# Loading the quarters of x and the first gate pair's weights during the attention heads

## The chip, the cores and the metric

The kernel runs on one core of one Trainium2 chip. The metric is the device time of the program in microseconds. TensorE (PE) multiplies, with its weight loads shown apart (PEld); VectorE (DVE), ScalarE (ACT) and GpSimd (POOL) compute elementwise; SyncE (SP) issues most of the DMAs, POOL some.

## The reference

One DeepNorm decoder layer in float32: 512 tokens, width 1024. A combined projection gives q, k, v (8 heads of 64), the input p of a pool mixer and the gates of two branches:

```python
proj = h @ w_in[l]
q, k, v, p, g = jnp.split(proj, [...], axis=-1)
y_attn = moba_attention(q.reshape(hs), k.reshape(hs), v.reshape(hs), rel_bias) @ w_branch_attn[l]
y_pool = multiscale_pool(p, w_pool_group[l], pool_scale[l]) @ w_branch_pool[l]
gates = jax.nn.sigmoid(g.astype(jnp.float32)).astype(h.dtype).reshape(B, S, N_BRANCHES, D)
mixed = gates[:, :, 0] * y_attn + gates[:, :, 1] * y_pool
h = layer_norm(ALPHA * h + mixed @ w_out[l], ln1_g[l], ln1_b[l])
a, u = jnp.split(h @ w_ffn_in[l], 2, axis=-1)
a = causal_dwconv(a, conv_w[l], conv_b[l])
f = (jax.nn.gelu(a, approximate=False) * u) @ w_ffn_out[l]
h = layer_norm(ALPHA * h + f, ln2_g[l], ln2_b[l])
```

The attention adds a relative bias per head and is causal. The change lies in the part that computes the gates and in the attention heads ahead of it; nothing of the mathematics differs.

## The kernel before, in words

Activations are kept transposed, channels on the partitions: x^T is eight tiles of 128 x 512. A product in float32 is made of three passes in a reduced type (`mm3`, L243 to L247): high x high, low x high, high x low. The high and low parts of a weight or an activation come from `split` (L72 to L78): ACT copies the high part (L76), DVE subtracts it (L77).

Many of the projections are done in pairs of output tiles by seven block products instead of eight (`seven`, L285). For that the weights of a pair are needed as four tiles A, X, D and Y, made of sums of weights. `fetch_raw` (L176) loads A and D as they are, on SP (L180, L182); X is loaded plainly on SP (L188) and then the other weights are added to it by an accumulating DMA on POOL (L190). `fetch_seven` (L194) forms Y on DVE (L207) and splits each. The activations are needed as four sums of quarters of x^T, called nT1, T3, nT2 and T4: `t_form` (L261) makes one of them in place of a quarter on DVE (L264 or L267) and, where it is told to, splits it. The weights of later chunks are fetched three chunks ahead; a pair's X and D are loaded into "homes", places that a small function gives for each pair. A home is free for the next load when the split of the pair that had it is done.

The order of the program is this:

- Input projections, in pairs, and the pool mixer. q and k of two heads each are copied out of the accumulators into the tiles `rq` and `rk` (three buffers of each).
- Eight heads (loop at L650). In step h the key and query of head h + 2 are prepared (`head`), a product that has nothing to do with heads is done as filler (`in_tile` for h < 4, a branch product `early_branch` after that, copied by DVE at L646), the scores of head h + 2 are computed (`scores`), every second step two finished heads are multiplied with v (`pv`, tile `ob`), and the probabilities of head h are transposed (`trans`, L616, with copies to `PT` on ACT and DVE, L618 to L620). In `scores` DVE finds the maxima (four instructions at L550 into `pp` and `nm`, negated at L553), ACT takes the exponentials (L556), DVE the reciprocals of the sums (L558), and POOL scales the rows (L561).
- The branch stage (L684 on): the branch outputs, oT split into high and low, and ten branch products (`br_mm`). Here the four quarters of x^T are loaded once more by four DMAs on POOL into `quad0` to `quad3` (L689); the first gate pair's X and D are loaded into `oT`, which is no longer needed by then; from the third branch product on one sum of quarters per product is formed and split.
- Six gate pairs, f = 2 to 7, by `seven`; their tiles in the profile are `sag`, `sbg` and `scg`, and the split sums are `gT` and `gnT`. X of pair f has `quad1` or `quad3` for a home, in turn, D one half of `quad2`.
- The output projection, the first LayerNorm, the gated feed-forward part and the second LayerNorm.

The order of the instructions on each engine is set by the scheduler of the language, from the dependencies, from a timeline that it estimates and from places where the program says that something may be issued only after something else (`issue_after`). A line of the program therefore says little of the place at which it is issued. The change's line numbers are five higher than these in the part on the heads.

Of the kernel before, what the change touches and what calls it, by code (L numbers as in the profile page):

```python
# [14 lines left out]
P = 128  # L15
S = 512
# [36 lines left out]
def layer_kernel(ctx: ExitStack, tc: tile.TileContext, xT, x, w_v, w_c, rel_bias, invcnt, w_group,  # L53
# [18 lines left out]
    def split(hi, lo, src, copy=None):  # L72
        if copy:
            copy(hi, src)
        else:
            state["hi"] = nc.scalar.activation(hi, src, AF.Copy)  # L76
        state["lo"] = nc.vector.tensor_tensor(lo, src, hi.bitcast(F32), op=ALU.subtract)  # L77
        return state["lo"]  # L78
# [182 lines left out]
    def t_form(n, tt, b11, b12, b21, b22, cut=True, c=slice(0, 256)):  # L261
        if n in ("nT1", "T3"):
            v, a = {"nT1": (b11, b11), "T3": (b12, b22)}[n]
            nc.vector.tensor_tensor(v, a, b12, op=ALU.subtract)  # L264
        else:
            v, a = {"nT2": (b22, b11), "T4": (b21, b22)}[n]
            nc.vector.scalar_tensor_tensor(v, a, -1.0, v, op0=ALU.mult, op1=ALU.subtract)  # L267
        if cut:
            split(*(t[:, :, c] for t in tt[n]), v)
        return v  # L270
# [43 lines left out]

    keepp = ExitStack()
    zT = keepp.enter_context(tc.tile_pool(name="keepz", bufs=1)).tile([P, 4, S], F32, name="zT")
    attn = ExitStack()
    av = attn.enter_context(tc.tile_pool(name="av", bufs=3, side="right", reuse_waits="tile"))
    strips = {}
# [9 lines left out]
    nc.gpsimd.memset(eps_t, EPS)  # L329
    dummy = const.tile([P, 1], F32, name="dummy")  # L330
    nc.scalar.activation(dummy, eps_t, AF.Copy)
    warm = const.tile([P, S], mybir.dt.bfloat16, name="warm")
    nc.vector.memset(warm, 0.0)
    wb_ = bank("warm_ps")
    for i in range(WARM):
# [187 lines left out]
    second = in_tile("p", PLAIN[1])  # L523

    def heads_done(p, ba):
        raw_q[p] = av.tile([P, S], F32, tag="rq", name=f"rq{p}")
        state["copy"] = nc.scalar.activation(raw_q[p], ba, AF.Copy)

    Ps = {}
# [35 lines left out]
    for n in range(1 + pairs):  # L565
        if n == 0:
            u, done = xr[1][:, 3, :], lambda ba, u: pool_sum(0, ba)
        else:
            u = raw_k[n - 1] = av.tile([P, S], F32, tag="rk", name=f"rk{n - 1}")
            done = lambda ba, u, p=n - 1: heads_done(p, ba)  # L570
        seven(("i", n), (xT_hi, xT_lo), ti, xr[1][:, 2, n % 2 * 256:n % 2 * 256 + 256], u, done)
        if n == 0:
            behind_sum.close()
            pool_dif(PLAIN[0], state["Y"])
            pool_sum(PLAIN[1], second)
            with tc.issue_after(state["acc"].ins):
                write_table(table)
        elif n == 1:
            pool_out(PLAIN[0])
            pool_dif(PLAIN[1], state["add"])  # L580
            pool_dif(0, state["add"])
            pool_sum(1, xr[1][:, 3, :], -1.0)
            add1 = state["add"]
        elif n == 2:
            pool_out(PLAIN[1])
            pool_dif(1, add1)
            with tc.issue_after(state["acc"].ins):
                load_strip(0)
                load_strip(1)
            head(0, state["add"], state["copy"])  # L590
        elif n == 3:
            pool_out(0)
            pool_out(1)
            head(1, state["add"], state["copy"])
            pooling.close()
            aw = attn.enter_context(tc.tile_pool(name="aw", bufs=3, side="right", reuse_waits="tile"))
            scores(0)
# [46 lines left out]
    def early_branch(f):  # L644
        t = branch[f, 1] = gates[:, 2 * GSEVEN + f, :]
        nc.vector.tensor_copy(t, br_mm(f, 1))  # L646

    scores(1)
    with tc.issue_after(exps[0].ins):
        flush()  # L650
    for h in range(H):
        if h + 2 < H:
            head(h + 2, nms[h], exps[h])
        if h < 4:
            in_tile(*fill.pop(0))
        elif h < H - 1:
            early_branch(h - 4)
        if h + 2 < H:
            scores(h + 2)
        with ExitStack() as held:  # L660
            if h and h % 2 == 0:
                pv(h // 2 - 1)
                held.enter_context(tc.issue_after(state["pv"].ins))
            trans(h)
        if h < 4:
            with tc.issue_after(nms[h].ins), tc.issue_after(exps[h].ins):
                split(zT_hi[:, h, :], zT_lo[:, h, :], zT[:, h, :])
        if h == H - 1:
            early_branch(h - 4)
    pv(H // 2 - 1)  # L670
# [6 lines left out]
    more = bp.tile([P, 4, S], F32, name="more")  # L677
    for k in range(4):
        split(oT_hi[:, k, :], oT_lo[:, k, :], oT[:, k, :])
    gxs = ExitStack()  # L680
    gx = gxs.enter_context(tc.tile_pool(name="gx", bufs=1, reuse_waits="tile"))
    tg = {"nT1": tuple(gx.tile([P, 4, 256], F32R, name=f"gnT1_{q}") for q in ("hi", "lo"))}
    gx.tile([P, 256], F32, name="gx_gap")
    qraw = [gx.tile([P, D], F32, name=f"quad{n}") for n in range(4)]  # L684
    for n in parts[1:]:
        tg[n] = tuple(gx.tile([P, 4, 256], F32R, name=f"g{n}_{q}") for q in ("hi", "lo"))
    quads = [t.rearrange("p (k t) -> p k t", k=4) for t in qraw]
    for n, (k, t) in enumerate(((k1, t1), (k1, t2), (k2, t1), (k2, t2))):
        nc.gpsimd.dma_start(quads[n], xT[k.start * P:k.stop * P, t].rearrange("(k p) t -> p k t", p=P))  # L689
    state["limit"] = WO0 - 1  # L690
    mts = {}

# [1 line left out]
        nc.gpsimd.tensor_tensor(a, b, a, op=ALU.add)  # L694
        mts[f] = a

    homes["g", "X"] = lambda f: oT[:, 0:2, :].rearrange("p a c -> p (a c)")
    homes["g", "D"] = lambda f: oT[:, 2, :]
    for q in "XD":
        coming[q].remove(("g", GSEVEN))  # L700
        fetch_raw(("g", GSEVEN), q)
        homes.pop(("g", q))

    unused = [more[:, n, :] for n in range(4)]
    forms = list(parts)
    order = [(4, 1), (5, 1), (6, 1), (6, 0)] + [(f, 0) for f in range(6)]
    for n, (f, br) in enumerate(order):
        if f < GSEVEN:
            with tc.issue_after(state["o"].ins):
                for g in range(2):  # L710
                    nc.scalar.activation(gslot[8 * g + f], gslot[8 * g + f], AF.Sigmoid)
        b = br_mm(f, br)
        if f < GSEVEN:
            for t, v in ((gslot[8 + f], branch[f, 1]), (gslot[f], b)):
                nc.vector.tensor_tensor(t, t, v, op=ALU.mult)
            merged(f, gslot[f], gslot[8 + f])
            unused += [gslot[8 + f], branch[f, 1]]
        else:
            t = branch[f, br] = unused.pop(0)
            nc.scalar.activation(t, b, AF.Copy)  # L720
        if n >= 2 and forms:
            t_form(forms[0], tg, *quads)
            forms.pop(0)
            if not forms:
                homes["g", "X"] = lambda f: qraw[1 + 2 * (f % 2)]
                homes["g", "D"] = lambda f: qraw[2][:, f % 2 * S:(f % 2 + 1) * S]

    def gate_done(f, ba, u):
        if f < KT - 1:
# [20 lines left out]
              lambda ba, u, f=f: gate_done(f, ba, u), first_half if f == KT - 1 else None)  # L750
    bz = br_mm(f, 1, last_bank[0], range(2, 4), True)
    flush()
    gxs.close()
    ext = actp.enter_context(tc.tile_pool(name="ext", bufs=1, side="right"))
    mx_hi = act.tile([P, KT, S], F32R, tag="actT_hi", name="mx_hi")
    mx_lo = act.tile([P, KT, S], F32R, tag="actT_lo", name="mx_lo")
# [428 lines left out]
```

## Time and profile before

| | |
|---|---|
| median of the runs | 641.33 us (641.03 to 643.21, 3 runs) |
| profiled execution | 640.88 us |
| its span in the trace | 639.2 us, mean granted clock of TensorE 0.99 |
| TensorE busy | 619.3 us, 97% |
| DVE, ACT, POOL busy | 511.8, 361.5, 121.3 us |
| heads | about 85 to 150 us of the span |
| branch stage | about 150 to 181 us |
| first two gate pairs | about 181 to 210 us |

In the rows of a timeline the first number is the start within the span, the second the duration, both in microseconds; at the end stands, in brackets, how long the engine was idle before the instruction and what released it. A row with "x16" groups sixteen such instructions. "DMA to landing" is the time from an issue on an engine to the arrival of the data. The names in the trace are those of the program without their numbers: `quad`, `wraw`, `whi`, `wlo` stand for all tiles of that name. A window's row gives busy microseconds of each engine.

### The profile page before, as it was taken

What the parts mean: (1) busy time and instruction counts of PE and PEld (TensorE: products, weight loads), DVE (VectorE), ACT (ScalarE), POOL (GpSimd) and SP (SyncE); (2) the same over time, 40 slices, a digit from 0 to 9 for tenths busy, and PEclk for the clock granted to TensorE, in tenths of its full rate; (3) what the DMA queues carried; (4) which work ended last, traced back from release to release, by engine and by line L of the source; (5) the groups of instructions that cost most, each with busy time, mean ns of one, the idle gap of its engine ahead of it and who ended that gap; (6) DMA issues with size and microseconds to landing.
All of it is one profiled execution on the core that took longest, in us unless ns stands there. A gap on an engine that the chain in (4) does not pass through costs nothing.

```text
span 639.2 us, 10595 instructions
## 1 busy us (share of the span) xinstructions
PE 619.3 (97%) x4060; PEld 557.1 (87%) x4060; DVE 511.8 (80%) x790; ACT 361.5 (57%) x552; POOL 121.3 (19%) x133
## 2 busy tenths in 40 slices
PE   9999999999976999999999999999999999999994
PEld 6899998777866999888999999999999888888884
DVE  5988789773574887759897998899897959698885
ACT  6646687762652665505475665566656447555452
POOL 0134035331230312210102011011100302123202
PEclk9999999999997999999999999999999999999998
DMA  8576656520656744543927787777753995889805
GB/s 314 164 191 178 172 143 196 133 83 33 191 118 182 189 113 140 188 200 101 255 87 202 185 211 207 171 195 196 186 137 117 330 269 114 210 203 196 208 0 133
DMA packets 41636, 109.30 MB, mean 171 GB/s; under 512 B 4449, under 2 KB 4713, under 8 KB 41329
## 3 DMA queue, kind: packets, MB, share of 16 engines
q1 hardware_dynamic: 27808, 72.42, 34.1%
q0 software_dynamic: 13200, 35.15, 28.8%
q10 hardware_dynamic: 576, 1.05, 0.4%
q8 instruction: 32, 0.52, 0.3%
q14 instruction: 20, 0.16, 0.1%
HBM read 104.39 MB, written 3.17 MB: 168 GB/s over the span
## 4 chain that ended last, share of the span: by engine, by line
PE 89%; DMA 5%; DVE 3%; issue 1%; ACT 1%; POOL 0%; DVEq 0%; ACTq 0%; POOLq 0%
PE saf L243 5%; PE saf L246 5%; PE saf L247 5%; PE v L421 3%; PE fi L243 3%; PE fi L247 3%; PE fi L246 3%; DMA oT<-in_w_c 2%; PE sbf L246 2%; PE sbf L243 2%; PE sbf L247 2%; PE wo L246 2%; PE wo L243 2%; PE wo L247 2%; DMA quad<-in_w_c 2%; PE fod L243 2%
## 5 line engine op out<-in xcount | busy, mean ns | idle before, releaser
L77 DVE TENSOR_TENSOR wlo<-araw,whi 128x1024 fp32r<-128x1024 f32 x56 | 71.1, 1278 | 9.2 <-ACT whi L76 9.2
L76 ACT ACTIVATE whi<-araw 128x1024 fp32r<-128x1024 f32 x56 | 58.5, 1057 | 22.4 <-PE saf L246 5.1
L76 ACT ACTIVATE whi<-wraw 128x1024 fp32r<-128x1024 f32 (+1 forms) x49 | 49.7, 1019 | 35.8 <-DMA wraw<-in_w_fo 9.7
L77 DVE TENSOR_TENSOR wlo<-wraw,whi 128x1024 fp32r<-128x1024 f32 (+1 forms) x49 | 58.4, 1197 | 14.1 <-ACT whi L76 13.9
L190 POOL DMA_DIRECT2D xraw<-in_w_fi x15 | 18.1, 1206 | 135.2 <-DMA xraw<-in_w_fi 44.3
L76 ACT ACTIVATE whi<-tw 128x1024 fp32r<-128x1024 f32 (+1 forms) x30 | 29.4, 983 | 24.3 <-DMA tw<-in_w_fo 10.5
L77 DVE TENSOR_TENSOR wlo<-tw,whi 128x1024 fp32r<-128x1024 f32 (+1 forms) x30 | 33.4, 1129 | 7.7 <-ACT whi L76 7.7
L243 PE MATMUL saf<-nT_hi,whi 128*128 128x256 f32 x136 | 38.0, 280 | 0.3 <-ACT whi L76 0.2
L243 PE MATMUL saf<-hT_hi,whi 128*128 128x256 f32 x136 | 37.9, 279 | 0.1
L246 PE MATMUL sbf<-T_lo,whi 128*128 128x256 f32 x136 | 37.9, 279 | 0.0
L246 PE MATMUL saf<-nT_lo,whi 128*128 128x256 f32 x136 | 37.8, 278 | 0.0
L246 PE MATMUL saf<-hT_lo,whi 128*128 128x256 f32 x136 | 37.8, 278 | 0.0
L243 PE MATMUL sbf<-T_hi,whi 128*128 128x256 f32 x136 | 37.7, 278 | 0.0
L247 PE MATMUL saf<-nT_hi,wlo 128*128 128x256 f32 x136 | 37.7, 278 | 0.0
L247 PE MATMUL sbf<-T_hi,wlo 128*128 128x256 f32 x136 | 37.7, 277 | 0.0
L247 PE MATMUL saf<-hT_hi,wlo 128*128 128x256 f32 x136 | 37.7, 278 | 0.0
L247 PE MATMUL fi<-hT_hi,wlo 128*128 128x256 f32 (+1 forms) x112 | 36.2, 326 | 0.0
L246 PE MATMUL fi<-hT_lo,whi 128*128 128x256 f32 (+1 forms) x112 | 36.2, 325 | 0.0
L243 PE MATMUL fi<-hT_hi,whi 128*128 128x256 f32 (+1 forms) x112 | 36.1, 327 | 0.0
L561 POOL TENSOR_SCALAR pp<-pp,rs 128x128 f32<-128x128 f32 (+3 forms) x32 | 23.8, 759 | 30.7 <-DVE rs L558 27.2
L231 POOL DMA_DIRECT2D tw<-in_w_fo x18 | 15.6, 903 | 62.3 <-DVE wlo L77 60.7
L243 PEld LDWEIGHTS saf<-nT_hi,whi 128*128 128x128 f32 x136 | 25.5, 188 | 0.7 <-ACT whi L76 0.4
(353 smaller groups left out, 2212.6 us busy)
## 6 DMA issues: line engine op xcount, KB each, us to landing
tw<-in_w_fo POOLq DMA_DIRECT2D x20, 512.0 KB, 8.6
araw<-in_w_fi SPq DMA_DIRECT2D x17, 512.0 KB, 3.5
xraw<-in_w_fi SPq DMA_DIRECT2D x15, 512.0 KB, 4.0
xraw<-in_w_fi POOLq DMA_DIRECT2D x15, 512.0 KB, 6.7
araw<-in_w_c SPq DMA_DIRECT2D x11, 512.0 KB, 4.3
wraw<-in_w_fi SPq DMA_DIRECT2D x10, 512.0 KB, 4.1
wraw<-in_w_fo SPq DMA_DIRECT2D x10, 512.0 KB, 5.5
tw<-in_w_fo SPq DMA_DIRECT2D x10, 512.0 KB, 7.5
```

Source lines behind the costliest of these rows:

```text
L76: state["hi"] = nc.scalar.activation(hi, src, AF.Copy)
L77: state["lo"] = nc.vector.tensor_tensor(lo, src, hi.bitcast(F32), op=ALU.subtract)
L190: state["acc"] = nc.gpsimd.dma_start(v, bass.AP(tensor=a.tensor, offset=a.offset, ap=[[pst, pn], [u.offset + S - a.offset, 2], [est, S]]), ...
L231: nc.gpsimd.dma_start(raw, half(then[1:], sl), accum_op=ALU.add)
L243: ins = nc.tensor.matmul(out_, wh, ah, start=start, stop=False, **kw)
L246: nc.tensor.matmul(out_, wh, al, start=False, stop=False, **kw)
L247: nc.tensor.matmul(out_, wl, ah, start=False, stop=stop, **kw)
L421: ins = nc.tensor.matmul(bs[j], xs_[j][a], (wh, wl)[b], start=kt == 0 and n == 0, stop=False)
L561: nc.gpsimd.tensor_scalar(pp[:, offs[i]:offs[i] + n], pp[:, offs[i]:offs[i] + n], rs[:, i:i + 1], 1.0, op0=ALU.mult, op1=ALU.mult)
```

## The change

The four quarters and the first gate pair's X and D get a pool of their own, `gq`, that is there from before the heads until the end of the gates. The copies of q and k lie in the same four tiles until then: q of pair p in the first half of `quad p`, k in the second, so the tiles `rq` and `rk` are gone. A quarter can be loaded when the last head that reads its pair has done so. In the program the loads stand in step 5 of the loop over heads; the sums are formed, not split, in steps 6 and 7, two in each; in the branch stage only the splits are left, from the second branch product on. X has three homes in turn now, `gX`, `quad1` and `quad3`, and D has `gD` and the two halves of `quad2`.

```diff
+    quad = ExitStack()
+    gq = quad.enter_context(tc.tile_pool(name="gq", bufs=1, side="right", reuse_waits="tile"))
+    qraw = [gq.tile([P, D], F32, name=f"quad{n}") for n in range(4)]
+    quads = [t.rearrange("p (k t) -> p k t", k=4) for t in qraw]
+    gX, gD = gq.tile([P, D], F32, name="gX"), gq.tile([P, S], F32, name="gD")
...
-    warm = const.tile([P, S], mybir.dt.bfloat16, name="warm")
+    warm = pw.tile([P, S], mybir.dt.bfloat16, name="warm")
...
-        raw_q[p] = av.tile([P, S], F32, tag="rq", name=f"rq{p}")
+        raw_q[p] = qraw[p][:, :S]
...
-            u = raw_k[n - 1] = av.tile([P, S], F32, tag="rk", name=f"rk{n - 1}")
+            u = raw_k[n - 1] = qraw[n - 1][:, S:]
...
+    formed = []
     scores(1)
...
+        if h == 5:
+            for n, (k, t) in enumerate(((k1, t1), (k1, t2), (k2, t1), (k2, t2))):
+                nc.gpsimd.dma_start(quads[n], xT[k.start * P:k.stop * P, t].rearrange("(k p) t -> p k t", p=P))
+            homes["g", "X"], homes["g", "D"] = lambda f: gX, lambda f: gD
+            for q in "XD":
+                coming[q].remove(("g", GSEVEN))
+                fetch_raw(("g", GSEVEN), q)
+                homes.pop(("g", q))
+        if h >= H - 2:
+            formed += [t_form(name, None, *quads, cut=False) for name in parts[2 * (h - H + 2):2 * (h - H + 3)]]
         if h == H - 1:
             early_branch(h - 4)
...
-    qraw = [gx.tile([P, D], F32, name=f"quad{n}") for n in range(4)]
...
-    for n, (k, t) in enumerate(((k1, t1), (k1, t2), (k2, t1), (k2, t2))):
-        nc.gpsimd.dma_start(quads[n], xT[k.start * P:k.stop * P, t].rearrange("(k p) t -> p k t", p=P))
...
-    homes["g", "X"] = lambda f: oT[:, 0:2, :].rearrange("p a c -> p (a c)")
-    homes["g", "D"] = lambda f: oT[:, 2, :]
-    for q in "XD":
-        coming[q].remove(("g", GSEVEN))
-        fetch_raw(("g", GSEVEN), q)
-        homes.pop(("g", q))
...
-        if n >= 2 and forms:
-            t_form(forms[0], tg, *quads)
-            forms.pop(0)
+        if n and forms:
+            name, v = forms.pop(0)
+            split(*tg[name], v)
             if not forms:
-                homes["g", "X"] = lambda f: qraw[1 + 2 * (f % 2)]
-                homes["g", "D"] = lambda f: qraw[2][:, f % 2 * S:(f % 2 + 1) * S]
+                homes["g", "X"] = lambda f: (gX, qraw[1], qraw[3])[(f - GSEVEN) % 3]
+                homes["g", "D"] = lambda f: (gD, qraw[2][:, :S], qraw[2][:, S:])[(f - GSEVEN) % 3]
...
-    gxs.close()
+    quad.close()
```

How the scheduler has placed it is seen in the order of the instructions on the engines. On DVE, in the last heads, around the maxima of head 7 (`pp7`), before the change (`br1` and `br2` are early branch products, `PT5` and `PT6` the transposed probabilities of heads 5 and 6):

```order
L646 COPY gates_1091<-br1_1_1605 128x512
L550 ISA pp7_1619,nm7_1620<-sc7_01_1622,strip7_1463 128x128
...
L550 ISA pp7_1619,nm7_1620<-sc7_3_1624,strip7_1463 128x512
L550 ISA nm7_1620 128x1
L619 COPY PT5_1647<-tr5_1_1649 128x512
L620 COPY PT5_1647<-tr5_2_1650 128x256
L553 TENSOR_SCALAR nm7_1620<-nm7_1620 128x4
L646 COPY gates_1091<-br2_1_1670 128x512
L558 RECIPROCAL rs7_1621<-rs7_1621 128x4
L619 COPY PT6_1694<-tr6_1_1696 128x512
L620 COPY PT6_1694<-tr6_2_1697 128x256
```

The same place with the change:

```order
L651 COPY gates_1093<-br1_1_1606 128x512
L264 TENSOR_TENSOR quad1_83<-quad3_85,quad1_83 128x1024
L555 ISA pp7_1620,nm7_1621<-sc7_01_1623,strip7_1464 128x128
...
L267 SCALAR_TENSOR_TENSOR quad3_85<-quad0_82,quad3_85 128x1024
L624 COPY PT5_1648<-tr5_1_1650 128x512
L625 COPY PT5_1648<-tr5_2_1651 128x256
L558 TENSOR_SCALAR nm7_1621<-nm7_1621 128x4
L651 COPY gates_1093<-br2_1_1678 128x512
L267 SCALAR_TENSOR_TENSOR quad2_84<-quad3_85,quad2_84 128x1024
L624 COPY PT6_1702<-tr6_1_1704 128x512
L625 COPY PT6_1702<-tr6_2_1705 128x256
L563 RECIPROCAL rs7_1622<-rs7_1622 128x4
```

Three sums have come in, T3 (L264) ahead of the maxima, nT2 (L267 on `quad3`) behind them and T4 (L267 on `quad2`) ahead of the copies to `PT6`; the reciprocal of head 7 has gone from ahead of these copies to behind them.

The first sum, nT1, stands further ahead on DVE, with the change, among the work of head 2 and the copies of head 0:

```order
L555 ISA nm2_1187 128x1
L77 TENSOR_TENSOR wlo30_1244<-wraw30_1242,whi30_1243 128x1024
L264 TENSOR_TENSOR quad0_82<-quad0_82,quad1_83 128x1024
L624 COPY PT0_1214<-tr0_1_1216 128x512
L558 TENSOR_SCALAR nm2_1187<-nm2_1187 128x4
L625 COPY PT0_1214<-tr0_2_1217 128x256
```

Before the change the other five rows stand there in this order, without the sum. On POOL the loads of the quarters stand, with the change, between the scalings of the heads; `quad0` lies ahead of head 0's scaling and `quad1` behind head 1's, and the last two here:

```order
L378 DMA strip7_1464<-F_d_187 128x512
L676 DMA quad2_84<-in_xT 128x4x256
L566 TENSOR_SCALAR pp4_1366<-pp4_1366,rs4_1368 128x128
...
L566 TENSOR_SCALAR pp5_1466<-pp5_1466,rs5_1468 128x512
L676 DMA quad3_85<-in_xT 128x4x256
L566 TENSOR_SCALAR pp6_1542<-pp6_1542,rs6_1544 128x128
...
L566 TENSOR_SCALAR pp7_1620<-pp7_1620,rs7_1622 128x512
L190 DMA quad1_83<-in_w_c 128x2x512
```

Before the change the four loads follow each other behind head 7's scaling, ahead of the first accumulation of the gate pairs. On SP the plain load of the first gate pair's X into `gX` and that of D into `gD` stand at the beginning of the program now, between the loads of two weight tiles of the input projections; the accumulation into `gX` is POOL's first DMA.

More of the change, by code (lines that the diff above doesn't have):

```diff
@@ L679, in layer_kernel @@
         split(oT_hi[:, k, :], oT_lo[:, k, :], oT[:, k, :])
-    gxs = ExitStack()
-    gx = gxs.enter_context(tc.tile_pool(name="gx", bufs=1, reuse_waits="tile"))
+    gx = quad.enter_context(tc.tile_pool(name="gx", bufs=1, reuse_waits="tile"))
     tg = {"nT1": tuple(gx.tile([P, 4, 256], F32R, name=f"gnT1_{q}") for q in ("hi", "lo"))}
     gx.tile([P, 256], F32, name="gx_gap")
-    qraw = [gx.tile([P, D], F32, name=f"quad{n}") for n in range(4)]
     for n in parts[1:]:
         tg[n] = tuple(gx.tile([P, 4, 256], F32R, name=f"g{n}_{q}") for q in ("hi", "lo"))
-    quads = [t.rearrange("p (k t) -> p k t", k=4) for t in qraw]
-    for n, (k, t) in enumerate(((k1, t1), (k1, t2), (k2, t1), (k2, t2))):
-        nc.gpsimd.dma_start(quads[n], xT[k.start * P:k.stop * P, t].rearrange("(k p) t -> p k t", p=P))
     state["limit"] = WO0 - 1
@@ L695, in merged @@
         mts[f] = a
-    homes["g", "X"] = lambda f: oT[:, 0:2, :].rearrange("p a c -> p (a c)")
-    homes["g", "D"] = lambda f: oT[:, 2, :]
-    for q in "XD":
-        coming[q].remove(("g", GSEVEN))
-        fetch_raw(("g", GSEVEN), q)
-        homes.pop(("g", q))
     unused = [more[:, n, :] for n in range(4)]
-    forms = list(parts)
+    forms = list(zip(parts, formed))
     order = [(4, 1), (5, 1), (6, 1), (6, 0)] + [(f, 0) for f in range(6)]
```

## The prediction

> **What bounds the kernel now.** I read the shares first, then TensorE's waits around the stages that the change touches, then windows of 5 us through these stages.
>
> ```profile
> PE 619.3 (97%) x4060; PEld 557.1 (87%) x4060; DVE 511.8 (80%) x790; ACT 361.5 (57%) x552; POOL 121.3 (19%) x133
> PE sbg L243 <- ACT whi L76: 4.2, 1, 4.2
> PE sbg L247 <- DVE wlo L77: 3.0, 2, 1.9
> PE sag L247 <- DVE wlo L77: 2.0, 1, 2.0
> ```
>
> TensorE is busy 97% of 639.2 us, so only what makes it wait, or makes it wait anew, can show. The three lower rows are all its waits from 85 to 262 us, from the first heads into the gated pairs: 4.2 + 3.0 + 2.0 = 9.2 us, all in products of the gate pairs. The windows (span, busy time of PE, PEld, DVE, ACT and POOL, granted clock, DMA share, GB/s) say where:
>
> ```profile
> 180.00:185.00 5.00, 4.01 (x31) 3.65 (x29) 5.00 (x6) 4.79 (x7) 4.12 (x3) 1.00 0.34 105
> 185.00:190.00 5.00, 2.08 (x15) 1.86 (x15) 5.00 (x6) 2.50 (x5) 0.92 (x1) 1.00 0.73 116
> 190.00:195.00 5.00, 5.00 (x43) 5.00 (x44) 1.00 (x1) 0.38 (x1) 1.07 (x1) 1.00 0.84 291
> 195.00:200.00 5.00, 1.67 (x15) 1.47 (x13) 0.17 (x1) 0.24 (x1) 0.12 (x1) 0.95 0.68 120
> 200.00:205.00 5.00, 3.04 (x12) 2.74 (x13) 4.97 (x8) 4.12 (x6) 0.00 (x0) 0.50 0.20 63
> 205.00:210.00 5.00, 5.00 (x40) 5.00 (x39) 3.14 (x5) 1.79 (x4) 1.20 (x1) 0.87 0.66 209
> ...
> 215.00:220.00 5.00, 5.00 (x46) 5.00 (x45) 4.21 (x7) 2.73 (x6) 1.20 (x1) 1.00 0.82 188
> ```
>
> TensorE loses 9.2 of the 30 us from 180 to 210, and behind its longest wait the granted clock falls to a half. In the last heads it never waits; from 215 on the stage feeds itself, with DVE busy 4.21 of 5.
>
> **What the change takes away.** The causes, from the timelines of DVE, POOL, ACT and PE:
>
> ```profile
> 178.36 0.69 DVE L207 TENSOR_TENSOR araw<-oT,araw 128x512 f32<-128x512 f32 x1 [4.01 <-DMA oT<-in_w_c]
> 185.78 1.21 DVE L77 TENSOR_TENSOR gnT_lo<-quad,gnT_hi 128x1024 fp32r<-128x1024 f32 x1
> 193.93 1.20 POOL L190 DMA_DIRECT2D quad<-in_w_c  x1 [8.00 <-DMA quad<-in_w_c]
> 199.75 1.58 ACT L76 ACTIVATE whi<-quad 128x1024 fp32r<-128x1024 f32 x2 [7.98 <-DMA quad<-in_w_c]
> 200.87 0.58 PE L243 MATMUL sbg<-gT_hi,whi 128*128 128x256 f32 x1 [4.20 <-ACT whi L76]
> 203.14 0.41 PE L243 MATMUL sbg<-gT_hi,whi 128*128 128x256 f32 x1
> ...
> 206.34 0.28 PE L247 MATMUL sag<-gnT_hi,wlo 128*128 128x256 f32 x1
> 206.46 0.28 PE L243 MATMUL sag<-gnT_hi,whi 128*128 128x256 f32 x1
> ```
>
> *First pair (1.9 and 2.0 us of wait).* DVE sat 4.01 us until the sum for the first pair had landed in oT, then ran full from 178 to 190. Now that sum (gX) and gD are loaded at the start, and the four forms of 1.14 us (start to start, rows below), 4.6 us, have left the stage: DVE is 8.6 us ahead where it was 3.9 late. Both waits go.
>
> *Second pair (4.20 + 1.10 us).* Its X went into quad3, which is free only when the split at 185.78 ends (186.99): plain load, accumulation at 193.93, landing 199.75, 12.8 us in all. Now it goes to quad1, whose reader is the second split, one step of the branch loop after the first, some 20 us earlier. I take all of it as gone; what is left over for the load is about 12 us. Later pairs turn through three homes instead of two, so none gets tighter.
>
> *The half clock.* From 203.14 to 206.34 fifteen products start 0.213 us apart; the full-speed distance is the 0.12 us of the last two rows. 15 x (0.213 - 0.116) = 1.5 us, gone with the wait.
>
> Sum of the gain: 9.2 + 1.5 = **10.7 us**. The bound below is half of it, if the second pair's loads only move.
>
> **What the change adds: quad3 and two forms ahead of the last head's maxima.** T3 now stands in DVE's queue between the copy of an early branch (L646) and head 7's four maxima (L550), nT2 behind the maxima and ahead of the PT5 copies; the reciprocal for head 7 stands behind the PT6 copies. T3 reads quad3, whose DMA stands on POOL behind head 5's scaling.
>
> ```profile
> 132.46 3.00 POOL L561 TENSOR_SCALAR pp<-pp,rs 128x128 f32<-128x128 f32 x4 [5.53 <-DVE rs L558]
> 144.82 2.05 POOL L561 TENSOR_SCALAR pp<-pp,rs 128x128 f32<-128x128 f32 x4 [6.22 <-DVE rs L558]
> DMA to landing us min/median/max: 4.5/7.2/9.3
> 167.81 1.23 DVE L264 TENSOR_TENSOR quad<-quad,quad 128x1024 f32<-128x1024 f32 x1 [1.76 <-DMA quad<-in_xT]
> 168.95 0.69 DVE L715 TENSOR_TENSOR gates<-gates 128x512 f32<-128x512 f32 x1
> 137.21 0.69 DVE L646 COPY gates<-br 128x512 f32<-128x512 f32 x1 [0.76 <-PE br L247]
> 138.18 0.29 DVE L550 CUSTOM_DVE_ANT_0 pp<-sc,strip 128x128 f32<-128x128 f32 x1 [0.28 <-PE sc L547]
> 140.96 0.69 DVE L619 COPY PT<-tr 128x512 f32<-128x512 f32 x1
> 141.90 0.16 DVE L553 TENSOR_SCALAR nm<-nm 128x4 f32<-128x4 f32 x1
> 144.48 0.18 DVE L558 RECIPROCAL rs<-rs 128x4 f32<-128x4 f32 x1 [1.45 <-ACT pp L556]
> 145.66 0.69 DVE L619 COPY PT<-tr 128x512 f32<-128x512 f32 x1 [1.01 <-PE tr L616]
> 142.23 2.37 PE L629 MATMUL ob<-PT,vv 128*64 128x512 f32 x16
> 144.53 2.27 PE L616 MATMUL tr<-ident,pp 128*128 128x128 f32 x16
> 146.56 0.48 PE L243 MATMUL br<-zT_hi,whi 128*128 128x512 f32 x1
> ```
>
> The third row is from the four quad loads of now (issue to landing). They were issued together, 4.5 being the first; a lone one in the nearly idle stretch is nearest to that, so I take 4.5. Step by step:
> - Issue at 132.46 + 3.00 = 135.46, landing 140.0. DVE is free at 137.9 and waits 2.1 us. T3, 1.14 us: the maxima start at 141.1 (138.18 before).
> - The maxima with what lies in them take 140.96 - 138.18 = 2.78: 143.9. nT2: 145.0. The PT5 copies take 0.94 (140.96 to 141.90): 146.0, 4.1 late, and nm behind them too.
> - PE starts its ob products at 142.2, does the part that ACT's copy feeds, and waits from 142.7 to about 146.1, 3.5 us. Its transposes start at 148.0, not 144.53.
> - The PT6 copies follow the transposes by 1.13 (145.66 - 144.53) and take 1.0: 149.1 to 150.2. The reciprocal behind them: 150.2, not 144.48. POOL's scaling 0.34 later: 150.5, not 144.82, which is 5.7 late.
> - Six transposes of head 7 need that scaling and stand ahead of the branch product of 146.56. PE waits a second time, some 2 us, and that product starts at 152.2. **Loss 5.6 us.**
>
> The bounds: were quad3 there at once, T3, nT2 and the late reciprocal alone cost 3.4 (137.9 + 1.14 = 139.0, then the same steps: scaling at 148.2). From there each us that quad3 is later costs one us: with 7.2 to landing 8.3, with 9.3 10.4. T4 (1.14) stands where DVE waits for the transposes anyway: nothing.
>
> The Trainium skill, "DMA: Bandwidth & Descriptors", section "Anatomy of one DMA — SWDGE (gpsimd) path", gives such a transfer about 2.0 us fixed plus its bytes at 436 GB/s: an estimate of 3.2 us for 512 KB, with a loss of 4.3. The row with 4.5 to 9.3 speaks against it, and it stands under the third rival only.
>
> **Elsewhere in the heads: nothing.** nT1 waits for quad1, issued on POOL behind head 1's scaling:
>
> ```profile
> 95.43 4.49 POOL L561 TENSOR_SCALAR pp<-pp,rs 128x128 f32<-128x128 f32 x4 [2.99 <-DVE rs L558]
> 102.74 0.68 DVE L619 COPY PT<-tr 128x512 f32<-128x512 f32 x1
> 117.67 1.31 PE L616 MATMUL tr<-ident,pp 128*128 128x128 f32 x10
> 20.00:22.00 2.00, 2.00 (x11) 1.65 (x10) 2.00 (x3) 1.79 (x2) 0.00 (x0) 1.00 0.11 37
> 22.00:24.00 2.00, 2.00 (x10) 1.65 (x9) 2.00 (x3) 1.06 (x1) 0.00 (x0) 1.00 0.00 0
> ```
>
> Issue at 99.92, landing at 104.4 to 107.1 by 4.5 and 7.2, so DVE stops 1.7 to 4.4 us where it made the PT0 copies at 102.74. Behind it are nm(2), two splits and head 4's key. TensorE has projections without heads in them until the next transposes, and those that need the late head start only at 117.67: cost 0; with 9.3 to landing up to 0.9. gX and gD (0.77 MB) are put on SP ahead of weights of the projections; from 20 to 24 us the DMA engines are nearly idle (last two rows, 0.11 and 0.00), and at the 291 GB/s of the window from 190 they need 2.6 us: 0; at the 120 of the window from 195 it would be 6.4, and up to 2.4 late. The four quad issues take POOL 0.76 us each in its gaps: 0.
>
> **Sum.** 640.88 (profiled execution; span 639.2) - 10.7 + 5.6 = 635.8. The median of the runs, 641.33, lies 0.45 above that execution, so **636.2** for the median.
>
> **Rivals** (medians).
> - *Half clock in the heads.* The 3.5 us wait may be enough to drop the clock. For it: a wait of 4.2 did it. Against: 1.9 and 2.0 did not, and the wait is nearer to 4.2 but still shorter. Behind the 4.2 us wait it stayed half until 206.3, 5.4 us after PE's return; half of that lost is 2.7: **638.9**.
>
> The Trainium skill, "TensorE: Matmul & The Clock Gate", section "What's actually happening", puts the drop at one idle window of about 3.4 us that runs free. The trace's 4.2 and 2.0 agree with it; by it a wait of 3.5 seldom covers a whole window.
>
> - *quad3 is there earlier, or nearly.* Nothing loads the DMA queues at 135 us. Loss 3.4 to 4.3: **634.0 to 634.9**. Against: no quad load of now landed in under 4.5.
> - *The gate waits only move.* Another load (A, or a weight two pairs on) is late in place of quad3; half the gain stays: 641.33 - 5.3 + 5.6 = **641.6**. Against: from 215 us TensorE keeps up with the same loads.
> - *Slower: quad3 late and the clock dropped.* At 9.3 to landing PE waits 8.3 us at ob; loss 10.4 + 2.7 = 13.1: 641.33 - 10.7 + 13.1 = **643.7**. It decides from a landing of 9.6 us without the clock, of 6.9 with it. For it: the median of now is 7.2. Against: that is with four in a row.
>
> **Chances.** Forecast 0.52, half clock 0.19, early quad3 0.14, moved waits 0.08, slower 0.07. The forecast, the half-clock case and most of the early one (0.10) lie between 632.5 and 640.5, 0.81 in all: that is the range. One measurement tells about 0.5% (3.2 us) from no change: faster than 638.1 are the forecast, the early quad3 and a quarter of the half-clock case, 0.70; within, most of the others, 0.25; over 644.5, most of the last, 0.05.
>
> **What the profile after would show.** T3 starts at about 140 on DVE with some 2 us of idle time put to quad<-in_xT; a wait of 3.5 us of PE's ob products for DVE's PT copies and one of about 2 for POOL's scaling, with the next branch product at 152; windows of 5.00 for PE through the gate pairs with the clock at 1.00; the first gate product (180.84 now) at about 186.4. I am wrong if PE does not wait in the last heads, if the clock is 0.5 there, or if a gate product still waits for a weight.

## The result, and the profile after

The changed kernel takes 637.83 us in the median of 20 runs (633.43 to 643.44), the kernel before 641.02 us in 20 runs beside it; the ratio is 0.9943, with a 95% interval of 0.9921 to 0.9965. That is 0.6% faster, 3.2 us in the medians. The ratios here and below are of means, and leave out executions more than 1.5% above the fastest of their kernel. The forecast was 636.2 us, 0.8% faster.

The profiled execution after is one of 639.6 us with a span of 637.9, 1.8 us above the median. Its page and TensorE's waits between 85 and 262 us (microseconds in total, times, longest):

```profile
PE 622.7 (98%) x4060; PEld 558.9 (88%) x4060; DVE 514.2 (81%) x790; ACT 361.1 (57%) x552; POOL 120.3 (19%) x133
PE ob L634 <- DVE PT L624: 2.9, 1, 2.9
PE tr L621 <- POOL pp L566: 1.5, 1, 1.5
PE sc L551 <- DMA k<-k: 0.4, 1, 0.4
```

The waits of the gate pairs are gone, all three rows. In their place stand the two that the prediction named, ob for DVE's copies and the transposes for POOL's scaling, and a third that it did not name: the scores of a head wait for the copies of a key. The windows of 5 us through the last heads and the gate pairs (columns as before):

```profile
145.00:150.00 5.00, 2.67 (x11) 0.99 (x9) 5.00 (x12) 0.00 (x0) 0.00 (x0) 1.00 0.26 82
150.00:155.00 5.00, 4.34 (x20) 3.00 (x20) 2.92 (x6) 3.48 (x10) 0.00 (x0) 0.66 0.06 23
155.00:160.00 5.00, 3.33 (x11) 2.52 (x12) 0.83 (x3) 0.00 (x0) 2.05 (x4) 0.73 0.00 0
160.00:165.00 5.00, 5.00 (x21) 3.21 (x20) 2.16 (x3) 1.46 (x2) 0.00 (x0) 0.92 0.00 0
...
195.00:200.00 5.00, 5.00 (x46) 5.00 (x45) 3.41 (x4) 2.25 (x5) 1.20 (x1) 1.00 0.80 174
200.00:205.00 5.00, 5.00 (x46) 5.00 (x45) 2.57 (x5) 2.72 (x5) 0.24 (x1) 1.00 0.64 171
```

From 195 on TensorE runs through at the full clock, 46 products in each window. The price is in the upper four rows: TensorE idles and the granted clock falls to 0.66 and 0.73. The chain that makes it, on DVE, POOL and PE:

```profile
144.76 1.23 DVE L264 TENSOR_TENSOR quad<-quad,quad 128x1024 f32<-128x1024 f32 x1 [3.14 <-DMA quad<-in_xT]
150.56 2.82 PE L634 MATMUL ob<-PT,vv 128*64 128x384 f32 x10 [2.89 <-DVE PT L624]
155.99 2.05 POOL L566 TENSOR_SCALAR pp<-pp,rs 128x128 f32<-128x128 f32 x4 [13.79 <-DVE rs L563]
156.42 1.92 PE L621 MATMUL tr<-ident,pp 128*128 128x128 f32 x6 [1.52 <-POOL pp L566]
```

and, for the four loads of the quarters, issue to landing:

```profile
DMA to landing us min/median/max: 4.6/5.2/5.7
```

T3 waits 3.14 us for quad3, as forecast in kind; the ob products wait behind it, and run at half the clock when they come.

To add this up I set the start of the same product in the profile before against that in the other profiles: how much later (+) or earlier (-) it is, in us. Each column is one execution; the last four belong to runs told below.

| product (its start before) | after | after, second profile | forms behind the reciprocal | quarters in the branch stage | gX behind the last key |
|---|---|---|---|---|---|
| first input product behind v, p (26.72) | +2.71 | +0.31 | +0.42 | +0.49 | -0.26 |
| scores of head 5 (124.30) | +2.70 | +0.35 | +0.42 | +0.49 | -0.26 |
| third ob (142.23) | +3.72 | +1.61 | +1.58 | +0.49 | -0.26 |
| third early branch product (146.56) | +11.43 | +6.32 | +2.38 | +0.50 | -0.24 |
| first gate product (180.84) | +12.67 | +6.33 | +2.35 | +0.61 | -0.27 |
| third gate pair (213.99) | +0.32 | -6.02 | -9.99 | -11.74 | -12.61 |
| end of the span (639.2) | -1.3 | -7.2 | -11.7 | -13.4 | -14.3 |

So this execution lost 2.7 us at the very start, 1.0 at the key copies, 9.0 in the last heads (from +3.72 to +12.67), won 12.35 in the gate pairs and 1.6 behind them. The 1.6 us lie at the first pairs of the feed-forward part (345 to 352 us before); no run here was made for them. The loss at the start can be read from the windows from 5 to 10 us, of before and of after, where TensorE did half as many products in the same time (the profile before first):

```profile
5.00:10.00 5.00, 5.00 (x22) 3.81 (x21) 3.22 (x6) 2.75 (x4) 0.00 (x0) 1.00 0.95 360
```

```profile
5.00:10.00 5.00, 5.00 (x11) 3.21 (x10) 3.35 (x7) 3.29 (x6) 0.00 (x0) 1.00 0.95 371
```

The products of v are some 0.43 us apart there in the profile after and 0.23 in the profile before. Products of this size are 0.43 apart at the half clock, too (from 158.56 to 158.99 us of the profile after); but the granted clock reads 1.00 in both rows, so that the clock made this start slow is not shown.

### The profile page after: what moved, and what is told of

It reads as the page before. It is cut to its first block, busy times and chain, and to the rows that moved or that the text cites. A ratio compares the mean times of both kernels' runs of the same rounds, so it can differ in the third digit from the quotient of the medians.

```text
span 637.9 us, 10600 instructions
## 1 busy us (share of the span) xinstructions
PE 622.7 (98%) x4060; PEld 558.9 (88%) x4060; DVE 514.2 (81%) x790; ACT 361.1 (57%) x552; POOL 120.3 (19%) x133
## 4 chain that ended last, share of the span: by engine, by line
PE 94%; DMA 2%; DVE 1%; POOL 1%; issue 0%; ACT 0%; DVEq 0%; POOLq 0%; ACTq 0%
PE saf L243 5%; PE saf L247 5%; PE saf L246 5%; PE v L426 3%; PE fi L243 3%; PE fi L247 3%; PE fi L246 3%; PE sbf L243 2%; PE sbf L247 2%; PE sbf L246 2%; PE wo L247 2%; PE wo L246 2%; PE wo L243 2%; PE br L243 2%; PE br L246 2%; PE br L247 2%
## 5 line engine op out<-in xcount | busy, mean ns | idle before, releaser
L77 DVE TENSOR_TENSOR wlo<-araw,whi 128x1024 fp32r<-128x1024 f32 x56 | 68.2, 1226 | 10.9 <-ACT whi L76 10.4
L77 DVE TENSOR_TENSOR wlo<-wraw,whi 128x1024 fp32r<-128x1024 f32 (+1 forms) x49 | 58.4, 1197 | 11.7 <-ACT whi L76 11.5
L561 ACT ACTIVATE pp<-pp,nm 128x128 f32<-128x128 f32 (+3 forms) x32 | 17.6, 552 | 19.0 <-DVE nm L558 18.3
```

The source lines that it names most:

```text
L561: exps[h] = nc.scalar.activation(pp[:, offs[i]:offs[i] + n], pp[:, offs[i]:offs[i] + n], AF.Exp, bias=nm[:, i:i + 1], accum_out=rs[:, i:i ...
```

## The experiments

Ratios are to the kernel before, run beside it on the same chip, with 95% intervals; short diffs are against the changed kernel. The key instructions of the diffs are kept in variables by lines that are left out (`scaled[h]` is the last scaling of head h on POOL, `copied[h]` the copy of its key on SP, `state["rs"]` the reciprocal, `state["pt2"]` the last copy to PT). `issue_after` puts an instruction behind another on the same engine.

### The changed kernel once more

> The changed kernel once more, for a second profile and as the run to compare the others with: 0.994 of the kernel before. Two theories on the 2.70 us that its first profile lost at the start of the program, where TensorE ran its first products of v at a distance of 0.43 us instead of 0.23 until about 10 us. Theory S: loading gX and gD at the start causes it; then this profile shows 2.7 us there again. Rival: the clock's state at the start differs from execution to execution and has nothing to do with the change; then the loss here is anything between 0 and 2.7 us.

634.58 us (633.66 to 637.70, 6 runs), 0.9928 (0.9905 to 0.9950). TensorE's waits in this profile, and the window in which the other profile had a clock of 0.66:

```profile
PE ob L635 <- DVE PT L625: 1.7, 1, 1.7
PE tr L622 <- POOL pp L567: 1.5, 1, 1.5
...
PE sc L552 <- DMA k<-k: 0.7, 1, 0.7
```

```profile
150.00:155.00 5.00, 3.23 (x16) 2.41 (x16) 0.97 (x3) 0.99 (x3) 2.05 (x4) 1.00 0.00 0
```

The start was 0.31 us later than before, not 2.7. So loading gX at the start does not cost 2.7 us there as such; theory S falls for that loss, and what made the one start slow stays open. The heads:

```profile
141.50 1.23 DVE L265 TENSOR_TENSOR quad<-quad,quad 128x1024 f32<-128x1024 f32 x1 [2.01 <-DMA quad<-in_xT]
```

T3 waits 2.01 us instead of 3.14, ob 1.7 instead of 2.9, and the clock stays at 1.00. Counted as above the last heads cost 4.7 us here (+1.61 at the third ob, +6.33 at the first gate product) against 9.0 with the half clock. Both the forecast and its first rival happened, in two executions of the same program.

### The forms behind head 7's reciprocal

```diff
-        if h >= H - 2:
-            formed += [t_form(name, None, *quads, cut=False) for name in parts[2 * (h - H + 2):2 * (h - H + 3)]]
+        if h == H - 2:
+            formed.append(t_form(parts[0], None, *quads, cut=False))
+        if h == H - 1:
+            with tc.issue_after(state["rs"].ins):
+                formed += [t_form(name, None, *quads, cut=False) for name in parts[1:]]
```

> The changed kernel, with T3, nT2 and T4 formed behind head 7's reciprocal on DVE instead of ahead of its maxima; loads, homes and the first sum as in the changed kernel. Theory F: the 9 us that the last heads lost come from T3 waiting for quad3 ahead of the maxima, with nT2, the late reciprocal and the half clock behind that wait. Then TensorE waits for nothing at ob and at the transposes, the clock stays at 1.00 from 145 to 165 us, and the span is 9 us below the changed kernel's: about 629, 0.98 of before. Rival: the loads in the heads (quad2 and quad3 beside the copies of k and the weights) are what costs; then waits stay in the heads and it comes out above 0.99.

630.83 us (629.18 to 636.09, 6 runs), 0.9869 (0.9838 to 0.9900); span of the profile 627.5.

```profile
PE sc L551 <- DMA k<-k: 0.7, 1, 0.7
...
PE tr L621 <- POOL pp L566: 0.2, 1, 0.2
```

No wait at ob, 0.2 at the transposes, the clock at 1.00: between the third ob (+1.58) and the first gate product (+2.35) 0.8 us are lost, not 4.7 or 9.0. The place of T3 and nT2 ahead of DVE's work for the heads is the loss, as theory F said; the size of 9 us was that of the execution with the half clock. The rival's wait is there too, but it is the small one: 1.2 us at the key copies.

### The wait for quad3 alone

Here T3 is formed from quad2 in place of quad3, so this one sum, and what is computed from it, is not the reference's. The loads stand ahead of the scores of head 7 in the program here; on POOL they have the same places among the scalings.

```diff
+            formed = [t_form(parts[0], None, *quads, cut=False), quads[1]]
+            with tc.issue_after(state["early"].ins):
+                state["T3"] = nc.vector.tensor_tensor(quads[1], quads[2], quads[1], op=ALU.subtract)
...
+                if h == H - 1:
+                    held.enter_context(tc.issue_after(state["T3"].ins))
+                state["max"] = nc.vector.tensor_tensor_reduce(
...
+            with tc.issue_after(state["max"].ins):
+                formed += [t_form(name, None, *quads, cut=False) for name in parts[2:]]
```

> The changed kernel, with T3 formed from quad2 in place of quad3 (its values are therefore not those of the reference), at the same place on DVE, and nT2 behind the maxima as in the changed kernel: the forms stay in the last heads, and only the wait for quad3's landing is taken away. By the prediction's steps the loss there is then 3.4 us instead of 5.6: TensorE waits about 1.2 us at ob where the changed kernel waits 1.7 to 2.9, the clock stays full, and the time is 2 us below the changed kernel's, 0.989 to 0.990 of before. Rival: the wait for quad3 is all of the loss, DVE's own 1.14 us per form have cover; then no wait is left at ob or at the transposes.

636.89 us (630.85 to 641.36, 12 runs), 0.9921 (0.9892 to 0.9950). The time does not answer, because the profile has a wait in a place that the edit does not touch, in the first input pair:

```profile
PE sai L243 <- ACT whi L76: 4.3, 2, 4.1
PE tr L625 <- POOL pp L570: 1.5, 1, 1.5
...
PE ob L638 <- DVE PT L628: 0.2, 1, 0.2
```

The last heads answer all the same: from +7.84 at the third ob to +11.01 at the first gate product, 3.2 us, with 3.4 forecast for this case and 4.7 with the wait for quad3. T3 itself took 1.76 us here instead of 1.23, so the forms' place in DVE's queue accounts for 2.6 to 3.2 us of the loss of 4.7, and the wait for quad3 for the rest. The rival (the wait is all) falls: 1.5 us remain at the transposes.

The wait in the input pair comes from the load of gX. ACT's row and POOL's two, of this execution:

```profile
20.83 1.38 POOL L190 DMA_DIRECT2D gX<-in_w_c  x1 [19.43 <-DMA gX<-in_w_c]
30.34 1.22 POOL L190 DMA_DIRECT2D xr<-in_w_c  x1 [8.13 <-DMA xr<-in_w_c]
```

```profile
38.55 1.58 ACT L76 ACTIVATE whi<-xr 128x1024 fp32r<-128x1024 f32 x2 [5.32 <-DMA xr<-in_w_c]
```

In the second profile of the changed kernel these stand at 19.04, 28.32 and 34.81:

```profile
19.04 1.38 POOL L191 DMA_DIRECT2D gX<-in_w_c  x1 [17.64 <-DMA gX<-in_w_c]
28.32 1.22 POOL L191 DMA_DIRECT2D xr<-in_w_c  x1 [7.90 <-DVE iT_lo L78]
...
34.81 1.58 ACT L77 ACTIVATE whi<-xr 128x1024 fp32r<-128x1024 f32 x2 [1.54 <-DMA xr<-in_w_c]
```

Here each is later, by 1.8, 2.0 and 3.7 us, and TensorE waits 4.1 us. That one delay causes the next fits the order of the rows, but they alone do not show it.

### gX and gD in the middle of the heads

```diff
-            for q in "XD":
-                coming[q].remove(("g", GSEVEN))
...
+            with tc.issue_after(copied[4].ins), tc.issue_after(scaled[3].ins):
+                for q in "XD":
+                    coming[q].remove(("g", GSEVEN))
...
```

> The changed kernel, with gX and gD loaded in the heads (behind the copy of head 4's key on SP, the accumulation behind head 3's scaling on POOL) instead of at the start. Theory S: the start is as fast as before and 2.7 us are won, 0.990 of before. Rival (the state of the clock at the start is chance): same as the changed kernel within 1 us in the median, and the start of a single profile may be fast or slow.

639.24 us (637.30 to 642.84, 12 runs), 0.9984 (0.9966 to 1.0002). Neither: it is 4.7 us slower than the changed kernel run beside it (634.58), and its start, with gX out of it, was 0.85 us later than before.

```profile
PE sc L553 <- DMA k<-k: 5.7, 1, 5.7
```

```profile
quad<-in_xT POOLq DMA_DIRECT2D x1, 512.0 KB, 12.1
```

```profile
135.00:140.00 5.00, 3.86 (x12) 2.53 (x14) 2.23 (x10) 0.22 (x1) 0.18 (x1) 0.50 0.19 53
```

The first row is of TensorE's waits, the second of the DMA issues between 110 and 140 us with the time to landing in the last column, the third a window. With gX's accumulation, a strip of the bias and quad2 issued behind each other from 122.4 on, quad2 took 12.1 us (4.6 to 5.7 in the profile after), and the scores of head 6 waited 5.7 us for the copies of a key that were issued behind it. The second of these copies landed 9.4 us after its issue, against 2.2 in the profile before; the DMA share was 0.94 or more from 129 to 134 us. The clock fell to 0.50. This is the third wait of the profile after, enlarged: small copies that TensorE waits for soon, beside large loads that have time.

### The quarters loaded and formed in the branch stage

```diff
-            for n, (k, t) in enumerate(((k1, t1), (k1, t2), (k2, t1), (k2, t2))):
-                nc.gpsimd.dma_start(quads[n], ...)
...
+    with tc.issue_after(scaled[H - 1].ins):
+        for n, (k, t) in enumerate(((k1, t1), (k1, t2), (k2, t1), (k2, t2))):
+            nc.gpsimd.dma_start(quads[n], ...)
...
-        if n and forms:
-            name, v = forms.pop(0)
-            split(*tg[name], v)
+        if n >= 2 and forms:
+            with tc.issue_after(state["pt2"].ins):
+                t_form(forms.pop(0), tg, *quads)
```

> The changed kernel, with the quarters loaded behind head 7's scaling and formed and split in the branch stage, as before the change; gX and gD at the start and the three homes stay. If the 12 us won in the gate pairs come from the homes and from the early load of the first pair's weights, the waits at 186, 190 and 201 us are gone here too, the heads lose nothing, and the time is 0.981 to 0.985 of before. If DVE needs the sums out of the branch stage, the two waits of the first pair (3.9 us) come back: 0.987 to 0.991.

> The kernel with the quarters loaded behind the heads and formed in the branch stage (homes and early gX, gD kept), once more, since its profiled execution was far from its other times and cannot be read. It should repeat its time, 0.983 of before, and its profile should show the heads as in the kernel before (no wait at ob, at the transposes or at the copies of k) and no waits in the gate pairs.

628.54 us the first time, 0.9827 (0.9797 to 0.9856); 627.99 (627.32 to 628.90, 4 runs) the second, 0.9810 (0.9796 to 0.9825). One execution of the first time, the profiled one, took 1,600 us and tells nothing. All of TensorE's waits in the second profile, and two windows of the gate pairs:

```profile
PE warm_ps L342 <- DVE warm L339: 1.2, 1, 1.2
PE v L423 <- DMA wraw<-in_w_v: 0.4, 1, 0.4
```

```profile
185.00:190.00 5.00, 5.00 (x45) 5.00 (x44) 1.42 (x2) 1.67 (x5) 0.67 (x1) 1.00 0.79 140
...
195.00:200.00 5.00, 5.00 (x46) 5.00 (x45) 4.86 (x7) 2.84 (x5) 1.28 (x1) 1.00 0.97 205
```

The two waits are those of the program's first 5 us. Nothing is lost between 26.72 (+0.49) and the first gate product (+0.61), at the keys neither, and the gate pairs win 12.35 us as in the changed kernel. So forming the sums in the heads buys nothing: DVE has the time for them in the branch stage.

### Two homes again

```diff
-                homes["g", "X"] = lambda f: (gX, qraw[1], qraw[3])[(f - GSEVEN) % 3]
-                homes["g", "D"] = lambda f: (gD, qraw[2][:, :S], qraw[2][:, S:])[(f - GSEVEN) % 3]
+                homes["g", "X"] = lambda f: qraw[1 + 2 * (f % 2)]
+                homes["g", "D"] = lambda f: qraw[2][:, f % 2 * S:(f % 2 + 1) * S]
```

on top of the edit before.

> The same, but with two homes in turn as before the change (X in quad3, quad1, quad3, ..., D in the halves of quad2): of the change only the early load of the first pair's X and D is left. The prediction laid the second pair's wait (4.20 + 1.10 us and the half clock behind it) to the home quad3, which came free too late. If the home is the cause, that wait is back, some 7 us, and the time is 0.993 to 0.995 of before. Rival: quad3 was free late only because DVE had waited for the first pair's X; with gX early the two homes do, no wait comes back, and the time is that of the run with three homes, 0.983.

> The kernel with only gX and gD early, at the start, once more: lowest times about 627, and about one time in five 4 us or more above them.

628.23 us (626.90 to 635.84, 6 runs), 0.9846 (0.9806 to 0.9887), and 627.51 (626.79 to 627.82, 5 runs), 0.9786 (0.9768 to 0.9805). No wait comes back; the gate pairs win 12.34 us (+0.01 to -12.33). That its X goes to quad3 was not enough to make the second pair wait. quad3 is again the home here, and ACT has that sum long before 195 us:

```profile
146.85 3.04 POOL L701 DMA_DIRECT2D quad<-in_xT  x4
168.22 1.23 DVE L77 TENSOR_TENSOR gnT_lo<-quad,gnT_hi 128x1024 fp32r<-128x1024 f32 x1 [0.26 <-ACT gnT_hi L76]
183.72 1.06 ACT L76 ACTIVATE whi<-quad 128x1024 fp32r<-128x1024 f32 x1 [0.89 <-PE scg L246]
```

The split that frees quad3 starts at 168.22 instead of 185.78. Two things could make that: DVE no longer waits 4.01 us for the first pair's sum, and the four loads are issued at 146.85 instead of 160.27, because the quarters have a place of their own and need not wait for the heads' tiles to be given back. In the profile before, the loads waited for the last ob products:

```profile
160.27 3.03 POOL L689 DMA_DIRECT2D quad<-in_xT  x4 [13.40 <-PE ob L629]
```

No run takes these two apart. In the changed kernel, too, the split that frees quad3 (`gnT_lo`) starts only 1.1 us behind the one that frees quad1 (`gT_lo`), so moving X from quad3 to quad1 can have won little:

```profile
177.20 1.22 DVE L77 TENSOR_TENSOR gT_lo<-quad,gT_hi 128x1024 fp32r<-128x1024 f32 x1
178.34 1.22 DVE L77 TENSOR_TENSOR gnT_lo<-quad,gnT_hi 128x1024 fp32r<-128x1024 f32 x1
```

### gX and gD behind the last key

The kernel with three homes and the quarters in the branch stage, and:

```diff
+            with tc.issue_after(copied[7].ins), tc.issue_after(scaled[6].ins):
+                for q in "XD":
+                    coming[q].remove(("g", GSEVEN))
...
```

> The kernel with the quarters loaded and formed in the branch stage and three homes, with gX and gD loaded behind the copies of head 7's key on SP (the accumulation behind head 6's scaling on POOL) instead of at the start. Theory: the load of gX at the start fits between the weights of the input pairs in most executions and in some does not (in one profile the accumulation came 1.8 us later, the weights of an input pair landed at 38.5 instead of 34.8 us, and TensorE waited 4.1 us); that makes the wide spread of the kernels that load it there. Then this one, which loads it where the DMA engines are nearly idle and no key is copied any more, has no wait there, nor at the copies of k, and all its times lie within 1.5 us of each other, at about 0.981 of before. Rival: the spread has another cause; then times some 5 us above the lowest remain.

> The kernel with gX and gD behind the copies of head 7's key once more, for the spread of its times beside the next on one chip: all within 1.5 us if the load at the start makes the high times, else some 4 us or more above the lowest.

627.04 us (626.63 to 627.99, 5 runs), 0.9788 (0.9773 to 0.9803), and 627.33 (627.11 to 627.62, 4 runs), 0.9786 (0.9769 to 0.9804). The loads lie where the theory wanted them:

```profile
133.75 0.58 SPq L188 DMA_DIRECT2D gX<-in_w_c  x1
138.62 1.27 POOL L190 DMA_DIRECT2D gX<-in_w_c  x1 [0.31 <-DMA gX<-in_w_c]
144.58 2.05 POOL L568 TENSOR_SCALAR pp<-pp,rs 128x128 f32<-128x128 f32 x4 [4.69 <-DVE rs L565]
```

No wait in the heads or the gates, and nine times within 1.4 us. It is 2.1% below the kernel before and, by the ratios, some 9 to 10 us below the changed kernel. No kernel of the study is faster; the one with two homes and gX at the start was as fast the second time (0.9786). That the load at the start makes high times is not shown by this: the second run with gX at the start (626.79 to 627.82) had none either, and the first had 632.46 and 635.84 in six.

### One more load into gX at the start

```diff
+            nc.sync.dma_start(gX, pair_of["g", GSEVEN][1])
```

on top of the kernel with two homes.

> The kernel with only gX and gD early (two homes), with one more load of 512 KB into gX at the start ahead of its own, so that gX's accumulation comes some 4 us later. By the same theory the late accumulation now meets the loads of the input pair's weights in every execution: TensorE waits at the first input pair near 42 to 46 us for ACT's copy of these weights, 3 to 5 us and the half clock behind it, and the median is 5 to 8 us above the kernel without the second load (628.2). Rival: the load at the start has nothing to do with the spread; same time as without it, and no wait there.

628.62 us (627.61 to 634.24, 6 runs), 0.9819 (0.9791 to 0.9847). A miss: the accumulation came at 23.59 instead of 19.04, and no input pair waited.

```profile
23.59 1.38 POOL L190 DMA_DIRECT2D gX<-in_w_c  x1 [22.19 <-DMA gX<-in_w_c]
28.36 1.22 POOL L190 DMA_DIRECT2D xr<-in_w_c  x1 [3.40 <-PE v L247]
```

A later accumulation alone does not bring the wait of 4.1 us. What did in that one execution is open.

### The quarters' loads alone in the heads

The forms behind head 7's reciprocal, and gX and gD behind the last key; of the loads in the heads only the quarters' remain.

> The changed kernel's early loads of the quarters, between the scalings of the heads, with the forms behind head 7's reciprocal and gX and gD behind the copies of head 7's key. Against the run with everything loaded behind the heads (627.0) this keeps only the quarters' early loads. If quad2's load beside the copies of head 6's key costs the 1.0 to 1.3 us that the profiles of the changed kernel and of its variants show there, that offset is here too, near 130 us, and the median is 628 to 629. If that offset came from gX at the start, it is gone: 627.

629.75 us (629.23 to 631.17, 4 runs), 0.9827 (0.9807 to 0.9847), 2.4 us above the kernel with everything behind the heads run beside it (627.33).

```profile
PE sc L553 <- DMA k<-k: 0.9, 1, 0.9
```

The copies of head 6's key are issued behind quad2 and a weight tile; that of kl landed 4.9 us after its issue here and 2.2 in the profile before. The offset is there without gX at the start: +0.05 at the scores of head 5, +1.15 at those of head 6 and +1.49 at the transposes of head 5 behind them. It comes with the quarters' loads in the heads, here 1.4 us; the weight tile, too, is issued 1.1 us nearer to the copies than before, and what that adds no run shows; another 0.8 is lost between the third ob (+1.49) and the first gate product (+2.27), as where the forms stood behind the reciprocal.

## Why the prediction was right, and where its steps were not

The sign and the size held: 0.6% faster, 0.8% forecast, and 637.83 us inside the range of 632.5 to 640.5. Four terms make the sum, and they were not all met; the number came out in part by luck. In the second profile the terms come to 7.2 us less than before, where 5.1 were forecast: the gain was larger than the sum had it, 1.2 us were won in the feed-forward part that it did not have, and losses of 1.6 at the start and at the key copies were missing from it. The half clock in the heads, a rival and not the forecast, costs 4.3 us more where it comes, and so brings the number back towards the forecast.

How often it comes is not shown, but each execution's mean granted clock is a hint: 0.990 in the profile with the half clock in the heads, 0.996 in the one without. Of the 20 executions of the result 12 lie at 0.990 or below and 4 at 0.995 or above, so the half clock was probably the common case there, and the median lies between the forecast (636.2) and that rival (638.9). When the kernel was run once more, with a median of 634.58, all six lay at 0.993 or above. By the prediction's own signs, too, the first profile goes against it (the clock is 0.5 in the last heads, the first gate product comes at 193.51), and the second agrees with it (T3 at 141.50, no half clock, the first gate product at 187.17, forecast 186.4).

**The gain, forecast 10.7 us, measured 12.35** in the profile after and within 0.01 us of that in the other profiles of the table. The step that was too small is the reading of the waits. I added idle times (9.2) and the loss to the half clock from 203.14 on (1.5). Counted from start to start the first pair lost 2.17 and 2.30 us around its two waits, where a product follows the next by 0.12, 4.2 in all and not 3.9, and the products between 200.87 and 203.14 ran at half clock too.

**The second pair's wait went, but not for the reason given.** "quad3 ... is free only when the split at 185.78 ends" was read rightly, but not why that split was so late. With two homes the wait is gone as well. The three homes of the change, and the step that gave them 4.20 + 1.10 us, bring nothing; what brings the gain is that the splits come early.

**The loss in the last heads, forecast 5.6 us: the mechanism is right, and the size holds without the clock.** Measured are 4.7 us in one execution, with T3 waiting 2.01 us (forecast 2.1) and a second wait of 1.5 at the transposes (forecast some 2). ob waited 1.7, not 3.5: it does more of its products before it needs the late copies than the step gave it. The case without the wait, 3.4, was measured as 3.2. In the other profile quad3 landed later, ob waited 2.9, and the first rival took place: the half clock, for 9.0 us in all. I gave that rival 0.19 with a wait of 3.5 us in mind; 2.89 were followed by the drop, 1.74 were not.

**"Elsewhere in the heads: nothing" was wrong by 1.0 to 1.5 us.** I counted the four loads by what POOL spends to issue them and by what waits for them, and not by what they delay on the DMA engines. The copies of head 6's key are issued behind quad2 and a weight tile and land later than before, and TensorE waits for them.

**"gX and gD at the start: 0, up to 2.4 late" held in most profiles** (from 0.1 us early to 0.8 late there) but not in one, where an input pair waited 4.1 us; and the profile after lost 2.7 us there, which another profile of the same kernel did not. The sum of the profile after (+2.7 + 1.0 + 9.0 - 12.35 - 1.6 = -1.3) is thus further from the forecast than the median is; with the second profile's terms (+0.3 + 1.3 + 4.7 - 12.35 - 1.2) it is -7.2, its span being 632.0.

The rival by which the gate waits only move did not come: no profile of any variant that can be read has a wait in the gate pairs.

## What to carry to other kernels

Before work is moved into an earlier stage because an engine has idle time there, see what stands behind it in that engine's queue: the forms cost 4.6 us of DVE, which was free, and up to 9 us of TensorE, which waited for the instructions behind them. Loads that have time (quad2 was issued at 124.55 us and read at 151.42) should not be issued just ahead of small copies that the bound engine needs within 4 to 5 us; 512 KB in the wrong place cost 1.0 to 1.4 us, two such loads and a strip a wait of 5.7, and behind the last copy nothing was lost. Where a buffer comes free too late, ask first why its reader is late: a place of its own for the quarters and an early first load together were worth all of the gain here, and the third buffer none.

## What the runs showed of the hardware

A TensorE wait of 2.89 us was followed by a drop of the granted clock to half; waits of 1.74, 1.90 and 2.02 us were not. The Trainium skill, "TensorE: Matmul & The Clock Gate", section "What's actually happening", speaks of an idle window of about 3.4 us; the trace shows the drop after less. The delay is not fixed: in the run with gX in the middle of the heads a wait of 5.70 us began at 130.44 and the clock was 1.00 up to 133 and 0.57 from 133 to 134, a drop some 2.7 us after the start; in the run without the wait for quad3 one of 4.08 us began at 42.37, and the clock was 1.00 up to 46 and 0.78 from 46 to 47, a drop some 4.2 us after the start. Behind the drop in the profile after the clock was 0.50 in the window from 151 to 152 us and 1.00 again at 155, and a second wait, of 1.52 us up to 156.42, was followed by another drop within a microsecond, while in the second profile the same wait of 1.52 us, with no drop ahead of it, was not (windows of 1 us of the profile after, columns as before):

```profile
151.00:152.00 1.00, 1.00 (x7) 0.76 (x4) 1.00 (x2) 0.99 (x5) 0.00 (x0) 0.50 0.00 0
155.00:156.00 1.00, 0.00 (x0) 0.00 (x0) 0.83 (x3) 0.00 (x0) 0.01 (x1) 1.00 0.00 0
157.00:158.00 1.00, 0.88 (x6) 0.64 (x6) 0.00 (x0) 0.00 (x0) 1.00 (x2) 0.67 0.00 0
```

Two executions of one program differ by 4 us in one stage with 1.2 us between them in a single wait.
